# Splitting three output stores by partition count in a one-core tree-attention kernel

## The chip, the core and the metric

The kernel runs on one core of a Trainium2 chip. The metric is the time of one execution on the device in microseconds (us): the median of the runs of a kernel. Beside the plain runs there is one profiled execution, from which all views of the profile come.

## What is computed

Inputs are Q, K and V of shape 8 x 12 x 512 x 64 in float32, so 96 heads of 512 rows of 64 numbers. The output has the same shape and type.

```python
mask[i, j] = 1 where j is i or an ancestor of i in a binary tree   # parent = (i - 1) // 2
scores = einsum('bhqd,bhkd->bhqk', Q, K) / sqrt(64) + (1 - mask) * (-1e9)
weights = exp(scores - max(scores));  weights /= sum(weights) + 1e-10
return einsum('bhqk,bhkd->bhqd', weights, V)
```

## The kernel before

The 96 heads are worked through in 48 pairs (`NP` = 48). The main loop runs over i from 0 to 48. For each pair, TensorE transposes Q and K (`turn`), makes two sets of scores (`scores1`, `scores2`), ScalarE takes their exponentials, TensorE multiplies with V (`values`), and VectorE divides by the row sums into an output tile (`norm`, the instructions of line 693). All of this is written out by hand in one order per engine; there is no scheduler.

An output tile `of` holds eight heads, 128 partitions and 4 x 64 float32 numbers (1 KB) for each head and partition. From pair 16 on, pair i holds heads 8 * (i // 4) + i % 4 and that number plus 4. So pairs 36 to 39 fill the tile of heads 72 to 79, pairs 40 to 43 that of heads 80 to 87, and pairs 44 to 47 that of heads 88 to 95.

The loads and most of the stores are issued by GpSimd (POOL) through its software queue, q0 in the profile. They are listed in `pool_program` and issued in that order as soon as `ready` allows. The loads come first. The stores follow in steps of eight heads, 1 MB each. For the tile of heads 72 to 79, POOL stores only heads 72 to 75 (512 KB); the store of heads 80 to 87 (1 MB) is its last.

SyncE (SP) issues the other stores through a hardware queue, q1 in the profile:

- after step i = 41 (`APART_AT`), heads 76 to 79 (`APART`), which the change's name calls pairs 38 and 39 by size: 4 heads, 512 KB, in two stores of 60 and 68 partitions, that is 240 KB and 272 KB (`store_apart`, line 711);
- after steps 45, 46 and 47, the heads of pairs 44, 45 and 46: 256 KB each, all 128 partitions (line 885);
- at the end, one head of pair 47 (128 KB, line 887). Its other head is stored by ScalarE through its own hardware queue, q10 (line 888).

Every store goes through the helper `store`, so all have line 701 in the profile. Each waits for the VectorE instruction that wrote the last of its heads; the stores of one engine are issued in the order written. Every packet of q1 and of q10 that carries data is 1 KB: one head of one partition.

Of the kernel before, what the change touches and what calls it, by code (L numbers as in the profile page):

```python
# [119 lines left out]
def kernel(  # L120
# [7 lines left out]
    nc = tc.nc  # L128
    B, H, S, D = Q.shape
    P = nc.NUM_PARTITIONS  # L130
# [4 lines left out]
    NP = 2 * NQ  # L135
# [134 lines left out]
    def head(i, a):  # L270

        if i >= FAR:
            return 8 * (i // 4) + i % 4 + 4 * a
        return 2 * i + a if i < WIDE else 4 * (i // 2) + i % 2 + 2 * a
# [275 lines left out]
    def turn(name, i):  # L550
        pairs = range(i, i + (2 if i >= WIDE else 1))
        if name == "qst" and i >= FAR:
            pairs = range(i - i % 4, i - i % 4 + 4)
        assert all((name, head(j, a)) in issued for j in pairs for a in range(2)), (name, i)
        level = (i >= WIDE) + (i >= FAR)
        {"kst": (narrow_k, wide_k, wide_k), "qst": (narrow_q, wide_q, far_q)}[name][level](i)
        return i + (2 if i >= WIDE else 1)
# [4 lines left out]
    def scores1(i):  # L562

        sp = psS.tile([P, 2, 512], fp32, name="s1")
        for a in range(2):
            nc.tensor.matmul(  # L566
                out=sp[:, a, :],
                lhsT=(k1code if i < WIDE else k1wide)[64 * a:64 * a + CODE_ROWS, :],
                rhs=(q1code, q1wide, q1far)[(i >= WIDE) + (i >= FAR)][64 * a:64 * a + CODE_ROWS],
                start=True, stop=False,  # L570
            )
        for a in range(2):
            nc.tensor.matmul(  # L573
                out=sp[:, a, :], lhsT=keys(i, a, TOP),
                rhs=qTs[i][64 * a:64 * a + 64, :, :].rearrange("p t c -> p (t c)"),
                start=False, stop=True,
            )
        et = etpool.tile([P, 2, 4, 128], bf16, name="e1")
        nc.scalar.activation(  # L579
            out=et[:, :, :, :].rearrange("p a t c -> p (a t c)"),  # L580
            in_=sp[:, :, :].rearrange("p a c -> p (a c)"),
            func=AF.Exp, scale=scale,
        ) if i < WIDE else nc.scalar.activation(  # L583
            out=et[:, :, :, :].rearrange("p a t (r u) -> p a (t r) u", u=2 if i < FAR else 4),
            in_=sp[:, :, :].rearrange("p a (u c) -> p a c u", u=2 if i < FAR else 4),
            func=AF.Exp, scale=scale,
        )
        ets[i] = et
# [34 lines left out]
    def scores2(i):  # L623
        if i >= WIDE:
            return scores2_wide(i)
        sp = psS.tile([P, 2, 4, 128], fp32, name="s2")
        flat = sp[:, :, :, :].rearrange("p a t c -> p a (t c)")
        for a in range(2):
            nc.tensor.matmul(
                out=sp[:, a, :, 32:128], lhsT=k2code[64 * a:64 * a + CODE_ROWS, :],  # L630
                rhs=q2code[64 * a:64 * a + CODE_ROWS, :].rearrange(
                    "p (t c) -> p t c", t=4
                )[:, :, 32:128],
                start=True, stop=False,
            )
        for t, lo, hi in ((2, 32, 192), (0, 192, 256), (3, 288, 448), (1, 448, 512)):
            for a in range(2):
                nc.tensor.matmul(
                    out=flat[:, a, lo:hi], lhsT=keys(i, a, TILE2[t]),
                    rhs=qTs[i][64 * a:64 * a + 64, :, :].rearrange("p t c -> p (t c)")[:, lo:hi],  # L640
                    start=False, stop=t == 1, skip_group_check=t in (2, 3),
                )
        nc.scalar.activation(
            out=e2s[i % NE][:, :, :, 32:128].rearrange("p a t c -> p (a t) c"),
            in_=sp[:, :, :, 32:128].rearrange("p a t c -> p (a t) c"),
            func=AF.Exp, scale=scale,
        )

    def values(i):

        if i < NP - 1:
            obs[i] = ob = psO.tile([P, 2, 512], fp32, name="ob")
        else:
            obs[i] = ob = psS.tile([P, 2, 512], fp32, name="s1")
        e1, e2, vt = ets[i], e2s[i % NE], vts[(head(i, 0) // VB) % NV]

        vtile = VTILE if i < WIDE else WVTILE
        assert all(("vt", n, head(i, a)) in issued for n in PARTS[(i >= 8) + (i >= 16)] for a in range(2))

        def product(e, a, t, tile_v, lo=0, hi=128, **flags):  # L660
            nc.tensor.matmul(  # L661
                out=ob[lo:hi, a, 65 * t:65 * t + 65],
                lhsT=e[:, a, PLACE[t], lo:hi],
                rhs=vt[vtile[tile_v][0]][:, head(i, a) % VB, vtile[tile_v][1], 0:D + 1],
                **flags,
            )

        def halves(a):
            for t in (0, 1):
                product(e2, a, t, 1 + SELF[t], 0, 64, start=False, stop=t == 1)  # L670
                product(e2, a, t, 1 + t, 64, 128, start=False, stop=t == 1)

        for a in range(2):
            for t in range(4):
                product(e1, a, t, 0, start=t == 0, stop=False)
            for t in (2, 3):
                product(e2, a, t, 1 + t, start=False, stop=False)
            if i == NP - 1:
                halves(a)
        if i < NP - 1:  # L680
            for a in range(2):
                halves(a)

    def norm(i):
        j, r = divmod(i, 4)
        if r == 0:
            ofs[j] = opool.tile([P, 8, 4, D], fp32, name="of")
        o4 = obs[i][:, :, 0:260].rearrange("p a (t c) -> p a t c", c=D + 1)
        rec = small.tile([P, 2, 4, 1], fp32, name="rec")
        for a, n in ((0, 2),) if i < NP - 1 else ((0, 1), (1, 1)):  # L690
            nc.vector.reciprocal(out=rec[:, a:a + n, :, :], in_=o4[:, a:a + n, :, D:D + 1])  # L691
            h0, h1 = [head(i, x) % 8 for x in (a, a + n - 1)]
            nc.vector.tensor_tensor(  # L693
                out=ofs[j][:, h0:h1 + 1:head(i, 1) - head(i, 0), :, :],
                in0=o4[:, a:a + n, :, 0:D],
                in1=rec[:, a:a + n, :, :].to_broadcast([P, n, 4, D]),
                op=ALU.mult,
            )

    def store(eng, h0, n, step=1, p0=0, p1=P):  # L700
        return eng.dma_start(  # L701
            out=Or[p0:p1, h0:h0 + step * (n - 1) + 1:step, :],
            in_=ofs[h0 // 8][p0:p1, h0 % 8:h0 % 8 + step * (n - 1) + 1:step, :, :].rearrange(
                "p h t d -> p h (t d)"
            ),
        )


    APART, APART_AT, APART_ROWS = 76, 41, 60

    def store_apart():

        for p0, p1 in ((0, APART_ROWS), (APART_ROWS, P)):
            store(nc.sync, APART, 4, 1, p0, p1)

    def pool_program():
# [135 lines left out]
    for i in range(NP + 1):  # L852
        steps = FIRST[i] if i < len(FIRST) else "SVK" if i % 2 else "SVQ"
        steps = "SQVK" if i == FAR - 1 else steps
        for step in steps:
            if step == "S" and i < NP:
                scores1(i)
                scores2(i)
            if step == "V" and i >= 1:
                values(i - 1)  # L860
                norm(i - 1)
                valued = True
            if step == "K" and kdone < NP:
                kdone = turn("kst", kdone)
            if step == "Q" and qdone < NP:
                qdone = turn("qst", qdone)
            if step == "W":
                nc.scalar.copy(
                    out=codes[64:64 + CODE_ROWS, 1280:1536], in_=codes[0:CODE_ROWS, 1280:1536]
                )  # L870
            if step == "X":
                spin("s1" if valued else "ob", 2)
            if step == "D":
                spread_by(nc.vector.tensor_copy, BY_VECTOR, STEADY_VECTOR, i)
            if step == "A":
                spread_by(nc.scalar.copy, BY_SCALAR, STEADY_SCALAR, i)
        if "D" not in steps:
            spread_by(nc.vector.tensor_copy, BY_VECTOR, STEADY_VECTOR, i)
        if "A" not in steps:
            spread_by(nc.scalar.copy, BY_SCALAR, STEADY_SCALAR, i)  # L880
        pool(i)
        if i == APART_AT:
            store_apart()
        if i >= NP - 3 and i < NP:
            store(nc.sync, head(i - 1, 0), 2, 4)
    assert not program
    store(nc.sync, head(NP - 1, 0), 1)
    store(nc.scalar, head(NP - 1, 1), 1)
# [30 lines left out]
```

## Time and profile before

| | us |
|---|---|
| median of 3 plain runs | 134.24 (134.17 to 134.83) |
| the profiled execution's own time | 135.14 |
| its span, first to last instruction | 133.4 |

The profiled execution took 0.90 us more than the median, and 1.7 us of its time lie outside the span. In the views, q0 is the queue of POOL's transfers (loads and stores), q1 that of SP, q10 that of ScalarE, and q8 and q14 fetch instructions. "DMA share" is the mean busy share of the core's 16 DMA engines. Packets are noted with a small overlap, so the share of a stretch in which all 16 work without a break can pass 1.

### The profile page before, as it was taken

The numbers are of one execution on the slowest core, as the hardware profiler recorded it, in microseconds if no ns is written. First come the engines' busy times: TensorE is split into PE (matmuls) and PEld (weight loads), VectorE is DVE, ScalarE is ACT, GpSimd is POOL, SyncE is SP. The second block draws the span as 40 slices with busy tenths as digits, with TensorE's granted clock in tenths as the row PEclk, the third lists the DMA queues.
The fourth block names the chain that finished last, engine by engine and source line by source line (L and its number), as shares of the span: only waits on it lengthen the run. The fifth ranks groups of instructions, "written<-read, shape, count | busy, mean of one in ns | idle before, by whom it ended". The sixth has DMA issues, their size and how long they took to land.

```text
span 133.4 us, 5419 instructions
## 1 busy us (share of the span) xinstructions
PE 112.9 (85%) x2350; PEld 79.2 (59%) x2353; DVE 105.2 (79%) x254; ACT 98.6 (74%) x159; POOL 85.0 (64%) x116
## 2 busy tenths in 40 slices
PE   6786989599899889899989898995999999999700
PEld 2343665467577567576757666763766777766500
DVE  3439779988999998889889699996999977783610
ACT  4359578579779796689976977974999778889500
POOL 6989639454573999995599999728998644002000
PEclk9999999999999999999999999999999999999955
DMA  2999999999999999999999999999999999999970
GB/s 97 243 179 195 201 196 200 201 206 202 200 204 211 202 209 204 210 207 202 208 205 205 341 231 204 333 241 288 287 248 325 220 360 402 403 397 367 356 266 14
DMA packets 28092, 32.25 MB, mean 242 GB/s; under 512 B 1149, under 2 KB 23293, under 8 KB 28069
## 3 DMA queue, kind: packets, MB, share of 16 engines
q0 software_dynamic: 25696, 29.63, 109.5%
q1 hardware_dynamic: 1813, 1.83, 4.0%
q10 hardware_dynamic: 560, 0.46, 1.1%
q8 instruction: 18, 0.29, 0.8%
q14 instruction: 5, 0.04, 0.1%
HBM read 37.94 MB, written 12.58 MB: 379 GB/s over the span
## 4 chain that ended last, share of the span: by engine, by line
DMA 29%; DVE 23%; POOL 19%; PE 18%; issue 5%; ACT 2%; POOLq 0%; ACTq 0%
DMA vst<-in_V_dram 15%; DMA qst<-in_Q_dram 14%; POOL vt L370 10%; DVE vt L370 8%; PE ob L661 7%; DVE of L693 6%; POOL kst L243 2%; PE s L566 2%; POOL qst L243 2%; DVE rec L691 2%; PE ktp L469 2%; PE s L573 1%; DVE kq L485 1%; ACT e L617 1%; PE s L600 1%
## 5 line engine op out<-in xcount | busy, mean ns | idle before, releaser
L583 ACT ACTIVATE e<-s 128x1024 bf16<-128x1024 f32 x40 | 40.9, 1023 | 16.1 <-PE s L573 15.8
L661 PE MATMUL ob<-vt,e 128*128 128x65 bf16 (+1 forms) x940 | 37.2, 197 | 2.0 <-DVE of L693 1.5
L661 PEld LDWEIGHTS <-e 128*128 128x128 bf16 (+1 forms) x960 | 30.2, 102 | 10.4 <-DVE of L693 2.2
L370 POOL COPY vt<-vst 32x512 int32<-32x512 int32 (+4 forms) x44 | 32.2, 733 | 4.9 <-PE ob L661 2.7
L617 ACT ACTIVATE e<-s 128x384 bf16<-128x384 f32 x80 | 34.7, 491 | 0.0
L693 DVE TENSOR_TENSOR of<-ob,rec 128x512 f32<-128x512 f32 x47 | 32.5, 691 | 1.6
L370 DVE COPY vt<-vst 32x1024 bf16<-32x1024 bf16 (+5 forms) x47 | 23.2, 493 | 3.0 <-DMA vst<-in_V_dram 2.2
L691 DVE RECIPROCAL rec<-ob 128x8 f32<-128x8 f32 x47 | 9.6, 204 | 10.2 <-PE ob L661 9.0
L701 POOL DMA_DIRECT2D out_dram<-of x11 | 9.8, 890 | 9.2 <-DVE of L693 8.8
L611 PEld LDWEIGHTS <-kq 64*128 64x128 bf16 x320 | 12.2, 94 | 5.2 <-issue 0.7
L573 PE MATMUL s<-qq,kq 64*128 64x512 bf16 x80 | 15.3, 377 | 0.0
L611 PE MATMUL s<-qq,kq 64*128 64x64 bf16 (+1 forms) x320 | 14.9, 208 | 0.4 <-issue 0.4
L566 PE MATMUL s<-far,codes 40*128 40x512 bf16 x64 | 12.5, 386 | 0.1
L579 ACT ACTIVATE e<-s 128x1024 bf16<-128x1024 f32 x8 | 8.2, 1022 | 5.9 <-PE s L573 5.9
L542 DVE COPY qq<-qtp 128x1024 bf16<-128x1024 bf16 x16 | 10.9, 681 | 1.4 <-PE qtp L537 1.4
L253 POOL DMA_DIRECT2D qst<-in_Q_dram x12 | 8.5, 705 | 4.7 <-DMA kst<-in_K_dram 1.8
L600 PEld LDWEIGHTS <-codes 40*128 40x128 bf16 x80 | 6.1, 95 | 8.7 <-issue 3.2
L370 ACT COPY vt<-vst 32x512 int32<-32x512 int32 (+3 forms) x19 | 10.4, 545 | 1.2 <-DMA vst<-in_V_dram 0.8
L476 PE MATMUL ktp<-ptile,kst 128*64 128x128 bf16 x256 | 10.1, 220 | 1.0 <-issue 0.6
L600 PE MATMUL s<-far,codes 40*128 40x384 bf16 x64 | 10.6, 324 | 0.4 <-ACT e L617 0.3
L253 POOL DMA_DIRECT2D kst<-in_K_dram x11 | 8.4, 762 | 3.6 <-DMA vst<-in_V_dram 1.9
L298 POOL DMA_DIRECT2D vst<-in_V_dram x7 | 5.8, 823 | 5.8 <-DMA vst<-in_V_dram 4.0
(56 smaller groups left out, 153.6 us busy)
## 6 DMA issues: line engine op xcount, KB each, us to landing
out_dram<-of POOLq DMA_DIRECT2D x10, 1024.0 KB, 15.8
kst<-in_K_dram POOLq DMA_DIRECT2D x9, 512.0 KB, 14.4
qst<-in_Q_dram POOLq DMA_DIRECT2D x8, 512.0 KB, 16.3
vst<-in_V_dram POOLq DMA_DIRECT2D x12, 256.0 KB, 13.5
vst<-in_V_dram POOLq DMA_DIRECT2D x6, 512.0 KB, 12.8
qst<-in_Q_dram POOLq DMA_DIRECT2D x6, 256.0 KB, 12.3
kst<-in_K_dram POOLq DMA_DIRECT2D x4, 256.0 KB, 9.7
out_dram<-of SPq DMA_DIRECT2D x3, 256.0 KB, 6.9
```

The costliest lines, as they stand in the source:

```text
L253: return nc.gpsimd.dma_start(out=kept[b][:, h0 % KB:h0 % KB + n, :, :].rearrange("p (g x) t d -> p g (x t d)", x=x), in_=src[:, h0 // x:(h ...
L370: return copy(out=dst, in_=src)
L542: nc.vector.tensor_copy(out=qqs[j][:, :, 8 * last:8 * last + 8, :].rearrange("p b u c -> p b (u c)"), in_=quarters,)
L566: nc.tensor.matmul(out=sp[:, a, :], lhsT=(k1code if i < WIDE else k1wide)[64 * a:64 * a + CODE_ROWS, :], rhs=(q1code, q1wide, q1far)[(i >= ...
L573: nc.tensor.matmul(out=sp[:, a, :], lhsT=keys(i, a, TOP), rhs=qTs[i][64 * a:64 * a + 64, :, :].rearrange("p t c -> p (t c)"), start=False, ...
L583: ) if i < WIDE else nc.scalar.activation(
L600: nc.tensor.matmul(out=flat[:, a, :, :].rearrange("p u (t c) -> p u t c", t=4)[:, :, :, 32 // n:], lhsT=k2wide[64 * a:64 * a + CODE_ROWS, ...
L611: nc.tensor.matmul(out=flat[:, a, :, lo:hi], lhsT=keys(i, a, WTILE2[t]), rhs=qT[64 * a:64 * a + 64, :, lo:hi], start=False, stop=t == 1, s ...
L617: nc.scalar.activation(out=e2s[i % NE][:, a, :, 32:128].rearrange("p t (r u) -> p t r u", u=n), in_=flat[:, a, :, :].rearrange("p u (t r) ...
L661: nc.tensor.matmul(out=ob[lo:hi, a, 65 * t:65 * t + 65], lhsT=e[:, a, PLACE[t], lo:hi], rhs=vt[vtile[tile_v][0]][:, head(i, a) % VB, vtile ...
L691: nc.vector.reciprocal(out=rec[:, a:a + n, :, :], in_=o4[:, a:a + n, :, D:D + 1])
L693: nc.vector.tensor_tensor(out=ofs[j][:, h0:h1 + 1:head(i, 1) - head(i, 0), :, :], in0=o4[:, a:a + n, :, 0:D], in1=rec[:, a:a + n, :, :].to ...
```

## The change

The store of heads 76 to 79 is issued by SP in three pieces of 36, 24 and 68 partitions in place of two of 60 and 68. The store of pair 44 is issued in two pieces of 108 and 20 partitions in place of one of 128. The bytes and the instructions of the other engines stay. SP issues eight stores in place of six. The transfers of the two hardware queues take eight completion semaphores in turn, and one that takes a semaphore for the second time first waits for the transfer that had it. With two more transfers these places shift by two: the store of 20 partitions and SP's three later stores each wait for one of the four transfers at the start of the kernel, and ScalarE's last store waits for the landing of the new store of 36 partitions.

```diff
-    APART, APART_AT, APART_ROWS = 76, 41, 60
+    APART, APART_AT, APART_ROWS = 76, 41, (36, 60, P)
 
     def store_apart():
 
-        for p0, p1 in ((0, APART_ROWS), (APART_ROWS, P)):
+        for p0, p1 in zip((0,) + APART_ROWS, APART_ROWS):
             store(nc.sync, APART, 4, 1, p0, p1)
...
         if i >= NP - 3 and i < NP:
-            store(nc.sync, head(i - 1, 0), 2, 4)
+            for p0, p1 in ((0, 108), (108, P)) if i == NP - 3 else ((0, P),):
+                store(nc.sync, head(i - 1, 0), 2, 4, p0, p1)
```

## The prediction

> **What bounds the kernel now.** I began with the table by stages, because the change touches only stores that are issued after 111 us. Its columns: the stretch, its length, busy us (and instructions) of PE, PEld, DVE, ACT and POOL, granted clock, DMA share, GB/s.
>
> ```profile
> 115.00:119.00 4.00, 3.93 (x79) 2.93 (x77) 3.07 (x8) 3.23 (x7) 0.00 (x0) 1.00 1.04 403
> 119.00:121.00 2.00, 1.82 (x36) 1.18 (x37) 0.87 (x2) 2.00 (x4) 0.80 (x1) 1.00 1.00 386
> 121.00:122.00 1.00, 1.00 (x18) 0.51 (x14) 0.88 (x2) 0.83 (x3) 0.11 (x1) 1.00 0.88 329
> 122.00:124.00 2.00, 1.88 (x40) 1.16 (x35) 0.92 (x3) 1.97 (x4) 0.00 (x0) 1.00 1.02 372
> 124.00:126.50 2.50, 1.86 (x44) 1.42 (x40) 1.46 (x5) 1.30 (x3) 0.00 (x0) 1.00 0.99 358
> 126.50:128.70 2.20, 0.00 (x0) 0.00 (x0) 0.56 (x3) 0.00 (x0) 0.00 (x0) 0.59 0.98 348
> 128.70:129.30 0.60, 0.00 (x0) 0.00 (x0) 0.00 (x0) 0.00 (x0) 0.00 (x0) 0.50 0.55 191
> 129.30:130.30 1.00, 0.00 (x0) 0.00 (x0) 0.00 (x0) 0.00 (x0) 0.00 (x0) 0.50 0.25 85
> 130.30:131.80 1.50, 0.00 (x0) 0.00 (x0) 0.00 (x0) 0.00 (x0) 0.00 (x0) 0.50 0.06 23
> 131.80:133.40 1.60, 0.00 (x0) 0.00 (x0) 0.00 (x0) 0.00 (x0) 0.00 (x0) 0.50 0.00 0
> ```
>
> The last columns carry the argument. The 16 DMA engines are full until 121, dip to 0.88 for one microsecond, and are nearly full again until 128.7. TensorE has nothing left from 126.5. Then the DMA share falls to 0.55, to 0.25, and to 0.06. One engine of 16 is 0.0625, so from 130.3 to 131.8 a single DMA engine works and all else has ended. The end of the kernel is the moment at which the most loaded DMA engine has written its last packet. In the last 1.6 us nothing moves: that is the landing and the closing of the program, which the change does not touch.
>
> The queue's own waits from 122 on say the same of SP:
>
> ```profile
> engine line waited for: us in total, times, longest us
> SPq L701 <- DVE of L693: 12.1, 3, 9.8
> SPq L914 <- DMA out_dram<-of: 4.5, 3, 2.1
> ```
>
> Line 914 is the end of the program. SP waits there for stores to land. Before that it waits for VectorE, and once for 9.8 us.
>
> Next, what each store is, and how long from issue to landing:
>
> ```profile
> out_dram<-of SPq DMA_DIRECT2D x3, 256.0 KB, 6.9
> ...
> out_dram<-of SPq DMA_DIRECT2D x1, 272.0 KB
> ...
> out_dram<-of SPq DMA_DIRECT2D x1, 240.0 KB, 7.9
> out_dram<-of SPq DMA_DIRECT2D x1, 128.0 KB, 5.5
> out_dram<-of ACTq DMA_DIRECT2D x1, 128.0 KB, 4.7
> ```
>
> The 240 KB store (60 partitions) was issued at 111.2 and landed 7.9 us later, at 119.1. The third of SP's stores, that of pair 44, waits for VectorE until 122 (the timeline's line further below). So all q1 packets between 119 and 121 belong to the store of 68 partitions, give or take one:
>
> ```profile
> q0 software_dynamic: 193, 0.73, 93.6%
> q1 hardware_dynamic: 42, 0.04, 6.0%
> ```
>
> These are packets, MB, and the share of 16 engines in those 2 us, 32 us of engine time. A q0 packet takes 93.6% of 32 over 193 = 0.155 us; a q1 packet 6.0% of 32 over 42 = 46 ns. An engine that takes the two queues in turn needs 0.20 us for one of each, so it writes 9.9 q1 packets in 2 us. Then 42 packets are the work of about four engines: the 68-partition store runs on four of them, 17 partitions and 68 KB each. Sixty-eight is not divisible by 16; its largest divisor up to 16 is 4. I take this as the pattern: a store runs on as many engines as the largest such divisor. The Trainium skill's page "DMA: Bandwidth & Descriptors", section "Why a DMA increments its semaphore by 16 and not by 1", states it as the rule, and adds that the hardware path takes the lowest-numbered engines; the trace agrees on four, and no row here names an engine.
>
> **The change, part by part.** By that pattern, in KB for each engine that takes part:
>
> - Heads 76 to 79 before: 60 partitions of 4 KB on 15 engines, 16 each; 68 on 4, 68 each. After: 36 on 12 engines, 12 each; 24 on 12, 8 each; 68 as before.
> - Pair 44 before: 128 partitions of 2 KB on 16 engines, 16 each. After: 108 on 12, 18 each; 20 on 10, 4 each.
>
> An engine that takes part in every piece carried 16 + 68 + 16 = 100 KB and now carries 12 + 8 + 68 + 18 + 4 = 110 KB: ten more packets. One that takes part in none of the new pieces loses 32 KB, or 16 KB if it had none of the 60-partition store. The change moves work from a few engines to most of the others.
>
> What is it worth? Only the engine that ends last counts. No row tells which it is. The four with the 68-partition store stand out: apart from that store all engines are given almost the same, and the 68 KB are 68 x 46 ns = 3.1 us of an engine's time. Other things spread the engines too, since that tail is single, not four wide. I take the last engine to be one of the four and to take part in every piece.
>
> An engine that works without a break until its end is later by what it is given more, in whatever order the queues take it. The price of a q1 packet, low end, from the engine that is alone at the end (130.3 to 131.8):
>
> ```profile
> DMA packets 37, 0.03 MB, mean 23 GB/s; under 512 B 4, under 2 KB 37, under 8 KB 37
> q1 hardware_dynamic: 28, 0.03, 4.9%
> q10 hardware_dynamic: 9, 0.01, 1.6%
> ```
>
> Four of the 37 are the small ones that report an end, so 33 packets of data in 1.5 us, 45 ns each. High end, from the crowded stretch 122.8 to 124.4, where these packets would be written:
>
> ```profile
> q1 hardware_dynamic: 106, 0.11, 23.0%
> ```
>
> That is 23.0% of 25.6 us over 106, 56 ns: beside other work some q1 packets are slowed. So ten packets cost 0.45 to 0.56 us. Part of the ten go out in the crowd, part behind it; I take 0.50 us.
>
> The two added issues cost SP time:
>
> ```profile
> L701 SPq DMA_DIRECT2D out_dram<-of x6: 360/485/996, 111.2 to 126.6; - x6
> ...
> 111.24 11.21 SPq L701 DMA_DIRECT2D out_dram<-of  x3
> ...
> 123.87 3.61 SPq L701 DMA_DIRECT2D out_dram<-of  x3
> ...
> 127.12 0.35 ACTq L701 DMA_DIRECT2D out_dram<-of  x1
> ```
>
> One is 0.36 to 1.0 us, 0.49 as a median; the lines of the timeline below it put the first three between 111.24 and 122.45 and the next at 123.87. The first lies ahead of SP's wait of 9.8 us for VectorE: it delays the 68-partition store's issue, which has q0's packets ahead of it anyway. The second follows pair 44's first piece, which is issued by 122.45, and lies ahead of SP's next wait for VectorE, until 123.87. Both are hidden; without that cover 0.5 us each, but the last store's issue is not what ends. The waits on reused semaphores are for transfers of the kernel's start, and ScalarE's last store, at 127.1, waits for the 36-partition store, which should land near 119 as the 240 KB store does. Cost nothing; if the 36-partition store landed after 127.1, ScalarE's store would be late by the rest.
>
> Sum: 10 packets x 50 ns = +0.50 us. The profiled execution, 135.14 with a span of 133.4, would become 135.64 and 133.9. The median is 134.24, 0.90 below that execution; the same addition gives 134.74 us.
>
> **The rivals.** *Faster: the last engine is among those that lose.* If the engine that ends alone takes part in none of the new pieces, it loses up to 32 packets x 45 ns = 1.44 us. Then the engines that were next decide. The row 129.3 to 130.3 (share 0.25, four engines' worth) says that they end near 130.3, 1.5 us before the last. If one of these takes part in every piece it ends at 130.3 + 0.45, so the gain is 131.8 - 130.75 = 1.05 us: 133.2. For it: a single late engine, where four have the 68 KB, may be late for a reason of its own. Against it: the extra load of the four. Decided by whether the last engine is given the new pieces.
>
> *Slower: the crowd.* Fewer engines take more, and a store of 108 partitions reads its rows through 12 engines in place of 16, while POOL's last megabyte is still being written. If that slows the last engine's packets by the 10 ns between the crowded row and the earlier one, for half of its 110 packets, 0.55 us come on top of the 0.50: 135.3. For it: the price did rise from 46 to 56 ns when the store of pair 44 joined. Against it: bytes and rows stay the same in all. It decides once q1 packets cost more than 56 ns from 122 to 126.5.
>
> *No change.* The smaller pieces may be spread over all 16 engines, or the last engine's end may be set by something else; then 134.2. The same page's section "Rules for kernel authors" calls two transfers to disjoint halves of the partitions not worth it, since they use the same engines; by that rule the time stays too, or pays only for the issues. Four engines for 68 partitions speak against reading it so here.
>
> **How the numbers follow.** About 0.5% (0.67 us) is what a measurement of this kernel can tell from no change. Forecast, 0.47: own range +0.3 to +0.9 (134.5 to 135.1), since the four engines' packets may cost more than 56 ns; of this 0.27 within 0.5% and 0.20 above. Faster, 0.29: 132.9 to 133.5, all counted as faster. Crowd, 0.19: 135.0 to 135.8, slower. No change, 0.05. So faster 0.29, same 0.32, slower 0.39. The range leaves out a tenth at each side: 133.1 to 135.6. The time is that of the likeliest case.
>
> **What would show it.** In the profile after, q1's bytes stay and the issue table shows stores of 144, 96, 272, 216 and 40 KB. Right: DMA share near 1 until 128.7 but a tail at 0.06 that lasts some 2 us and ends near 132.3; q1 at 46 to 56 ns. Wrong, rival one: the tail at 0.06 is gone or short and the span is near 132.4. Wrong, rival two: q1 above 56 ns from 122 to 126.5. If the 36-partition store is no longer in flight by 119 and the tail has not moved, the count of engines for each piece is wrong.

## The result and the profile after

The changed kernel took 135.43 us (median of 6, 135.27 to 135.61) and the kernel before 134.24 (134.08 to 134.83): ratio 1.0084, 95% interval 1.0064 to 1.0105. It is slower by 1.1 us, or 0.84%; the prediction was +0.50 us and 134.74. Single executions of the kernel before, and of the variants below, are at times longer by up to 4%, mostly with a lower granted clock, and each ratio leaves out executions more than 1.5% above the fastest of their kernel.

The profiled execution after took 135.32 us with a span of 133.5, almost the same as the one before (135.14 and 133.4). So the two profiles do not show the 1.1 us as a difference of spans, and they must not be subtracted. The table by stages of the kernel after says why (columns as before: stretch, length, busy us of PE, PEld, DVE, ACT, POOL, granted clock, DMA share, GB/s):

```profile
24.00:28.00 4.00, 3.06 (x44) 1.95 (x45) 3.35 (x10) 1.34 (x4) 1.59 (x3) 0.72 1.35 199
28.00:32.00 4.00, 3.73 (x84) 2.87 (x81) 2.60 (x8) 2.85 (x4) 1.91 (x3) 0.85 1.29 206
...
122.00:124.00 2.00, 1.84 (x36) 1.16 (x34) 0.79 (x3) 1.95 (x4) 0.91 (x1) 1.00 0.59 214
124.00:126.50 2.50, 2.38 (x48) 1.55 (x46) 1.35 (x3) 2.35 (x4) 0.00 (x0) 1.00 0.95 365
126.50:128.70 2.20, 1.79 (x40) 1.35 (x40) 1.23 (x4) 1.23 (x3) 0.00 (x0) 1.00 0.75 243
...
129.30:130.30 1.00, 0.00 (x0) 0.00 (x0) 0.22 (x1) 0.00 (x0) 0.00 (x0) 1.00 1.00 353
130.30:131.80 1.50, 0.00 (x0) 0.00 (x0) 0.00 (x0) 0.00 (x0) 0.00 (x0) 0.92 0.40 140
```

TensorE still works until after 126.5 here, where before it had ended by then. The DMA engines, full before from 122 on, are only 0.59 busy from 122 to 124: they wait for stores that are not yet issued. ScalarE's last store is issued at 129.6, before at 127.1. Part of the cause lies 100 us earlier: from 24 to 32 us TensorE's clock was granted at 0.72 and 0.85 in place of 1.00. The half clock that makes these shares lasted 2 x (0.28 + 0.15) x 4 = 3.4 us, which can cost TensorE at most half of that, 1.7 us. The seventh instruction of line 693 starts at 31.2 us before and at 32.8 after, 1.6 us later. The rest of the 2.4 us arose later, at full clock, and is not explained. The stores that the change touches are issued after 113 us, and by then the arithmetic is 2.4 us late already, so this cannot be their work. The next section shows that the half clock comes and goes.

The stores are split as intended:

```profile
out_dram<-of SPq DMA_DIRECT2D x1, 272.0 KB
...
out_dram<-of SPq DMA_DIRECT2D x1, 216.0 KB
out_dram<-of SPq DMA_DIRECT2D x1, 144.0 KB
...
out_dram<-of SPq DMA_DIRECT2D x1, 96.0 KB
...
out_dram<-of SPq DMA_DIRECT2D x1, 40.0 KB
```

How many engines carry the pieces can be counted. SP's stores are 1408 KB in both kernels, so they make 1408 packets of data. What q1 has beyond these are the small packets that report an end, 4 bytes each. From 108 us to the end, before and after:

```profile
q1 hardware_dynamic: 1491, 1.44, 16.6%
...
q1 hardware_dynamic: 1506, 1.44, 16.6%
```

That leaves 83 before, 15 + 4 + 4 x 16, and 98 after, 12 + 12 + 4 + 12 + 10 + 3 x 16: one for each engine of each store, with the numbers of engines that the prediction assumed. The sum comes out in the profiles of all the runs below too.

The issues of SP and of ScalarE, shortest, median and longest in ns, and the first and last:

```profile
L701 SPq DMA_DIRECT2D out_dram<-of x8: 304/396/2501, 113.7 to 129.0; - x8
L701 ACTq DMA_DIRECT2D out_dram<-of x1: 351/351/351, 129.6 to 129.6; - x1
```

SP's longest took 2.5 us, where before it was 1.0.

### The profile page after: what moved, and what is told of

It is laid out like the page before. It is cut to its first block, busy times and chain, and to the rows that moved or that the text cites. A ratio compares the mean times of both kernels' runs of the same rounds, so it can differ in the third digit from the quotient of the medians.

```text
span 133.5 us, 5425 instructions
## 1 busy us (share of the span) xinstructions
PE 114.7 (86%) x2353; PEld 80.2 (60%) x2353; DVE 105.5 (79%) x254; ACT 98.6 (74%) x159; POOL 85.2 (64%) x116
## 4 chain that ended last, share of the span: by engine, by line
PE 45%; DVE 25%; ACT 7%; DMA 7%; issue 7%; POOL 6%; ACTq 0%; POOLq 0%
PE ob L661 15%; DVE vt L370 9%; DMA vst<-in_V_dram 7%; DVE of L693 6%; PE s L566 6%; PE s L573 4%; ACT e L617 4%; PE s L611 4%; PE s L600 4%; PE ktp L476 4%; PE qtp L537 3%; ACT e L583 3%; POOL kst L243 2%; POOL qst L243 2%; DVE rec L691 2%
## 5 line engine op out<-in xcount | busy, mean ns | idle before, releaser
L661 PE MATMUL ob<-vt,e 128*128 128x65 bf16 (+1 forms) x940 | 37.8, 198 | 3.4 <-DVE of L693 1.4
L661 PEld LDWEIGHTS <-e 128*128 128x128 bf16 (+1 forms) x960 | 30.7, 103 | 11.5 <-issue 2.1
L611 PE MATMUL s<-qq,kq 64*128 64x160 bf16 (+1 forms) x320 | 14.8, 208 | 0.4 <-issue 0.4
L485 DVE COPY kq<-ktp 128x256 bf16<-128x256 bf16 x20 | 8.3, 416 | 2.3 <-PE ktp L476 2.2
```

Source lines behind the costliest of these rows:

```text
L611: nc.tensor.matmul(out=flat[:, a, :, lo:hi], lhsT=keys(i, a, WTILE2[t]), rhs=qT[64 * a:64 * a + 64, :, lo:hi], start=False, stop=t == 1, s ...
L661: nc.tensor.matmul(out=ob[lo:hi, a, 65 * t:65 * t + 65], lhsT=e[:, a, PLACE[t], lo:hi], rhs=vt[vtile[tile_v][0]][:, head(i, a) % VB, vtile ...
```

## The experiments

**The kernel before again, and the two halves.** Four kernels on one chip, beside the same runs of the kernel before (median 134.33). The first has no edit.

> The kernel before, unchanged, for a second profile of it and a ratio that should be 1. The two profiles differ in more than the stores: in the one after, TensorE's granted clock is 0.72 from 24 to 28 us in place of 1.00, and from there on all arithmetic is later, by 2.43 us at the end (ScalarE's last store is issued at 129.56 in place of 127.12). Theory 'bytes': the measured +1.19 us is the last DMA engine's ten more packets, +0.5, and something on top; then this profile repeats the first one's tail (last issue near 127.1, a DMA share of 0.06 for 1.5 us). Theory 'clock': the dip at 25 us comes and goes between executions of any of these kernels, and this profile may show it. Theory 'clock by program': the dip belongs to the changed program, and this profile shows none. Ratio 1.000 under all.

Ratio 0.9994 (0.9972 to 1.0016). The profiled execution, of 136.52 us, has half clock too, in an earlier place:

```profile
0.00:24.00 24.00, 18.79 (x248) 10.83 (x249) 14.15 (x42) 12.59 (x18) 18.63 (x28) 0.86 1.26 188
24.00:28.00 4.00, 3.90 (x86) 2.73 (x84) 3.85 (x10) 3.93 (x6) 1.52 (x3) 1.00 1.33 198
```

0.86 over 24 us is 2 x 0.14 x 24 = 6.7 us of half clock, about twice the 3.4 of the kernel after; it lies from 11.5 to 18.3 us, and a further 3.4 us at 0.50 follow from 49.1. Its last store was issued at 130.9. So the unchanged kernel has such windows too, and "clock by program" falls. The Trainium skill's page "TensorE: Matmul & The Clock Gate", section "Part 1: The HAM clock gate (the 'warmup' mystery)", describes a gate that watches TensorE over windows of about 3.4 us and halves the clock after an idle one; the lengths here agree with whole windows. But the windows ahead of the half clock are not idle here: TensorE was busy for 1.84 of 3.41 us ahead of it in the first profile after, and for 1.97 and 1.65 of 3.41 us in this one.

The first half of the change alone:

```diff
-    APART, APART_AT, APART_ROWS = 76, 41, 60
+    APART, APART_AT, APART_ROWS = 76, 41, (36, 60, P)
...
-        for p0, p1 in ((0, APART_ROWS), (APART_ROWS, P)):
+        for p0, p1 in zip((0,) + APART_ROWS, APART_ROWS):
```

> The store of heads 76 to 79 in 36, 24 and 68 partitions, that of pair 44 whole. Theory 'bytes': the last engine has 4 KB more (12 + 8 in place of 16), so +0.2 us, ratio 1.0015. Theory 'clock by program': if the dip at 25 us is in this profile, the time is near the changed kernel's, +1.2 us, ratio 1.009, and if it is not, near 1.000. Theory 'issue': one more store in a queue that waits anyway, nothing.

Ratio 1.0036 (1.0002 to 1.0070), +0.48 us. Its profiled execution has a dip as well, 0.86 and 0.71 from 24 to 32 us.

The second half alone:

```diff
-            store(nc.sync, head(i - 1, 0), 2, 4)
+            for p0, p1 in ((0, 108), (108, P)) if i == NP - 3 else ((0, P),):
+                store(nc.sync, head(i - 1, 0), 2, 4, p0, p1)
```

> The store of pair 44 in 108 and 20 partitions, that of heads 76 to 79 in 60 and 68. Theory 'bytes': the last engine has 6 KB more (18 + 4 in place of 16), so +0.3 us, ratio 1.002. Theory 'clock by program': +1.2 us with the dip in the profile, 0 without. Theory 'issue': the second piece's issue took 2.50 us in the profile of the changed kernel (from 124.83) where the others took 0.3 to 0.5; if that, and not the bytes, makes the end late, this kernel has the whole +1.2 us and the one with only heads 76 to 79 split has none.

Ratio 1.0044 (1.0017 to 1.0071), +0.59 us. Each half costs, and the two add up to the whole, 1.1 us. The intervals reach down to 0.03 and 0.23 us, so the 0.2 and 0.3 of the theory "bytes" are not excluded. Its profile, without a dip, is the nearest to the first one of the kernel before:

```profile
126.50:128.70 2.20, 0.00 (x0) 0.00 (x0) 0.38 (x1) 0.00 (x0) 0.00 (x0) 0.56 0.95 338
...
129.30:130.30 1.00, 0.00 (x0) 0.00 (x0) 0.00 (x0) 0.00 (x0) 0.00 (x0) 0.50 0.16 54
130.30:131.80 1.50, 0.00 (x0) 0.00 (x0) 0.00 (x0) 0.00 (x0) 0.00 (x0) 0.50 0.03 12
```

TensorE is done by 126.5 and one engine is alone at the end again, with less of a lag: 0.03 x 16 x 1.5 = 0.7 us after 130.3. This single execution (134.45 us) was shorter than that first one of before (135.14). One profile of each kernel does not rank changes of this size.

As many stores as in the changed kernel, which the diff is against, but the old bytes on each engine:

```diff
-    APART, APART_AT, APART_ROWS = 76, 41, (36, 60, P)
+    APART, APART_AT, APART_ROWS = 76, 41, (45, 60, P)
...
-            for p0, p1 in ((0, 108), (108, P)) if i == NP - 3 else ((0, P),):
+            for p0, p1 in ((0, 64), (64, P)) if i == NP - 3 else ((0, P),):
```

> As many stores as in the changed kernel, but each engine with the bytes it had before: heads 76 to 79 in 45, 15 and 68 partitions (12 + 4 in place of 16 KB on fifteen engines), pair 44 in 64 and 64 (8 + 8 in place of 16 KB on sixteen). Theory 'bytes': ratio 1.000. Theory 'issue' (the added stores, their waits and the later issues cost, not the bytes): near the changed kernel's 1.008. Theory 'clock by program': 1.000 or 1.009, with the dip's absence or presence in the profile.

Ratio 1.0009 (0.9990 to 1.0027). Two more stores, their waits on reused semaphores and the longer issues cost at most 0.36 us, and 0.1 as it was measured. SP's issues were stretched here as well:

```profile
L701 SPq DMA_DIRECT2D out_dram<-of x8: 350/623/1720, 113.8 to 129.2; - x8
```

So theory "issue" falls: it is how the pieces spread over the engines that costs, not that there are more of them. Pieces of 108 and 20 partitions differ from these in their shape as well as in KB for each engine, and the last experiment comes back to that.

**The changed kernel again, a steadier clock, and even bytes.** Beside runs of the kernel before with a median of 134.28. The first has no edit against the changed kernel.

> The changed kernel again, on the same chip and beside the same runs as the next three. So far it was 1.008 of the kernel before, the two halves alone 1.004 each, and the kernel with the same number of stores and the old bytes per engine 1.001. Theory 'bytes': 1.005 to 1.008 again. Theory 'clock' (the difference of the first two profiles, 2.43 us in the arithmetic, is chance: one execution with a window of half clock near 25 us, one without): the time of this kernel varies as much as that of the kernel before, and the window may lie elsewhere or be absent in this profile.

Ratio 1.0048 (1.0021 to 1.0076), +0.64 us. This profile has no dip, and the last store of ScalarE is issued at 128.2:

```profile
24.00:28.00 4.00, 2.72 (x62) 2.00 (x63) 3.72 (x11) 2.19 (x4) 2.10 (x4) 1.00 1.34 200
...
129.30:130.30 1.00, 0.00 (x0) 0.00 (x0) 0.00 (x0) 0.00 (x0) 0.00 (x0) 1.00 0.76 265
130.30:131.80 1.50, 0.00 (x0) 0.00 (x0) 0.00 (x0) 0.00 (x0) 0.00 (x0) 0.69 0.09 33
131.80:134.00 2.20, 0.00 (x0) 0.00 (x0) 0.00 (x0) 0.00 (x0) 0.00 (x0) 0.50 0.01 2
```

The clock is full, and the tail of about one engine is back: 0.09 in the stretch where before it was 0.06. In the last row one engine works on past 131.8, where before all was quiet; its last packet ends at 132.0, before at 131.8. Even without a dip the arithmetic is 1.1 us later here than in the first profile before (ScalarE's last store at 128.2 against 127.1), so this end is not the work of the change alone. The price of its q1 packets from 122 to 126.5:

```profile
q1 hardware_dynamic: 306, 0.31, 21.1%
```

21.1% of 72 us over 306 is 50 ns, as in the kernel before in the same stretch (26.8% over 383 packets).

Idle matmuls against the dips, in both kernels:

```diff
-    FIRST = ['KSQ', 'SXKQXDVAKQ', 'SVKQ', 'SKQAV', 'KSVXQA', 'SAKQVDW', 'SKDVQ', 'SVD', 'SVDKQX']
+    FIRST = ['KSQ', 'SXKQXDVAKQ', 'SXVKQX', 'SKXQAVX', 'KSVXQAX', 'SXAKQVDWX', 'SKXDVQX', 'SXVD', 'SVDKQX']
```

> The kernel before, with nine more pairs of idle matmuls on TensorE (step X) in the loop's steps 2 to 7, where windows of half clock were seen; all else is as before. Theory 'clock': the profile has a granted clock of 1.00 from 14 to 32 us, the last store is issued near 127 us, and the runs scatter less than those before (which go from 133.8 to 138.5); the median moves by less than 0.5 us. If the added matmuls are not hidden, the arithmetic comes up to 4 us later and the time rises by what is not absorbed by the loads.

> The changed kernel with the same added idle matmuls. Against the one before it this is the bytes alone, without the scatter of the clock, if the matmuls do what they are meant to. Theory 'bytes': later than the kernel of label e6_before_steady by 0.45 to 0.56 us if the price of the prediction holds (45 to 56 ns a packet), by 1.1 us if the measured price holds (110 ns). Theory 'clock': no difference between the two beyond 0.2 us.

Both missed. The profiles have a granted clock of 0.9 or more in every slice up to the end, but the added matmuls were not hidden: ratios 1.0461 (1.0409 to 1.0513) and 1.0497 (1.0441 to 1.0552) to the kernel before. Their ratios differ by 0.5 us, inside the width of either interval, so this pair says nothing on the change.

Even bytes:

```diff
-    APART, APART_AT, APART_ROWS = 76, 41, 60
+    APART, APART_AT, APART_ROWS = 76, 41, 64
```

> Heads 76 to 79 in 64 and 64 partitions, each on sixteen engines by the pattern: 32 KB on every engine, in place of 84 on four, 16 on eleven and 0 on one. Nothing else changes. If the four engines with the 68 KB end last (the prediction's choice), they lose 52 KB, 2.3 us at 45 ns, and the end falls to the next engines, which gain 16 or 32 KB, 0.7 to 1.4 us: by the first profile, where these end near 130.3, 131.0 to 131.7 in place of 131.8, so 0.1 to 0.8 us faster. If the last engine is another, it gains 16 KB or 32 KB: 0.7 to 1.4 us slower, and the prediction's choice was wrong.

Ratio 1.0025 (0.9996 to 1.0054). Neither forecast came out: +0.34 us (-0.05 to +0.73), no gain, and half of the smaller loss. The profile shows two late engines in place of one:

```profile
129.30:130.30 1.00, 0.00 (x0) 0.00 (x0) 0.00 (x0) 0.00 (x0) 0.00 (x0) 1.00 0.35 121
130.30:131.80 1.50, 0.00 (x0) 0.00 (x0) 0.00 (x0) 0.00 (x0) 0.00 (x0) 0.77 0.10 34
```

0.10 x 16 x 1.5 = 2.4 us of work after 130.3 is more than one engine can do in 1.5. With the same bytes on every engine some still end 1.5 us after the rest. So engines differ by something else than SP's stores, and taking the heavy load from four is of no use while others get 16 or 32 KB more. POOL's last store tells the same: two of its sixteen shares landed at 129.3 and 129.6, the other fourteen by 127.5.

**The dose, and a better split.** Beside runs of the kernel before with a median of 134.18. First, the changed kernel with its new split for three pairs:

```diff
-            for p0, p1 in ((0, 108), (108, P)) if i == NP - 3 else ((0, P),):
+            for p0, p1 in ((0, 108), (108, P)) if i <= NP - 1 else ((0, P),):
```

> The changed kernel, with the stores of pairs 45 and 46 in 108 and 20 partitions too: an engine that takes part in every piece gets 4 + 3 x 6 = 22 KB more than before in place of 10. This is the dose that the noise between executions does not cover. Theory 'bytes' at the prediction's price, 45 to 56 ns a packet: +1.0 to +1.2 us on the kernel before, ratio 1.0075 to 1.009. At twice that, as the first comparison of before and after looked: +2.4 us, 1.018. If the changed kernel's loss is from something else than the bytes of the loaded engines (the seven more issues of SP apart): near 1.005.

Ratio 1.0105 (1.0059 to 1.0151), +1.41 us for 22 KB: 64 ns for each KB, with 36 to 92 by the interval, so the 45 to 56 of the prediction are within it. (SP issues ten stores here, four more than the kernel before and not seven.)

Then, from the kernel before, all of heads 76 to 79 on four engines:

```diff
-    APART, APART_AT, APART_ROWS = 76, 41, 60
+    APART, APART_AT, APART_ROWS = 76, 41, 124
```

> Heads 76 to 79 in 124 and 4 partitions, both on four engines by the pattern (31 x 4 and 4 x 1): 128 KB on each of four engines in place of 84, nothing on the other twelve in place of 16 on eleven of them. Pair 44 is whole. Theory 'bytes', the last engine being one of the four: +44 KB at 45 to 56 ns, +2.0 to +2.5 us, ratio 1.015 to 1.018. If the last engine is one of the other twelve: faster by up to 0.7 us (16 KB) until the four overtake it.

Ratio 1.0125 (1.0073 to 1.0177), +1.68 us for 44 KB. The q1 packets from 119 to 121, and the end:

```profile
q1 hardware_dynamic: 40, 0.04, 5.8%
...
128.70:129.30 0.60, 0.00 (x0) 0.00 (x0) 0.00 (x0) 0.00 (x0) 0.00 (x0) 0.50 0.50 176
129.30:130.30 1.00, 0.00 (x0) 0.00 (x0) 0.00 (x0) 0.00 (x0) 0.00 (x0) 0.50 0.30 107
130.30:131.80 1.50, 0.00 (x0) 0.00 (x0) 0.00 (x0) 0.00 (x0) 0.00 (x0) 0.50 0.27 94
131.80:134.00 2.20, 0.00 (x0) 0.00 (x0) 0.00 (x0) 0.00 (x0) 0.00 (x0) 0.50 0.07 26
```

40 packets in 2 us, as for 68 partitions (42). The share is 0.27, four engines of 16 and a little, until 131.8: four engines end last, with the other twelve idle. One issue of SP is stretched as nowhere else:

```profile
L701 SPq DMA_DIRECT2D out_dram<-of x6: 286/1334/10277, 111.1 to 126.7; - x6
```

That of the four partitions, issued behind the 124, took 10.3 us. It goes to the four engines that still have the 124 KB each to write; that their queues were full is likely, but no view shows it.

Next, from the kernel before, a split that takes load from the four and gives none to four others:

```diff
-    APART, APART_AT, APART_ROWS = 76, 41, 60
+    APART, APART_AT, APART_ROWS = 76, 41, 108
```

> Heads 76 to 79 in 108 and 20 partitions: 36 + 8 = 44 KB on ten engines, 36 on two, nothing on four, in place of 84 on four, 16 on eleven, 0 on one. Pair 44 is whole. The kernel with 32 KB on all sixteen was no better than before, with two late engines in its profile in place of one. Theory 'one slow engine outside the loaded ones, and the four with 84': this relieves both, and the end falls to the engines between, which gain 28 KB, 1.3 us, on an end near 129.3 to 130.2 in the first profile: 130.6 to 131.5 in place of 131.8, so 0.3 to 1.2 us faster, ratio 0.991 to 0.998. Theory 'the engines between are late enough': same or up to 0.5 us slower.

Ratio 0.9951 (0.9921 to 0.9981): 133.56 us, faster than the kernel before by 0.66 us, and the best of all. The tail has gone:

```profile
128.70:129.30 0.60, 0.00 (x0) 0.00 (x0) 0.00 (x0) 0.00 (x0) 0.00 (x0) 1.00 0.82 285
129.30:130.30 1.00, 0.00 (x0) 0.00 (x0) 0.00 (x0) 0.00 (x0) 0.00 (x0) 0.67 0.14 46
130.30:131.80 1.50, 0.00 (x0) 0.00 (x0) 0.00 (x0) 0.00 (x0) 0.00 (x0) 0.50 0.00 0
```

All engines end within about 1 us, by 130.3, and the shares of POOL's last store end without a straggler (127.6 and 127.8 are the last two). Against even bytes (1.0025) it differs in the four engines that get nothing from heads 76 to 79, and in the 4 to 12 KB more on the others.

And the change's second half on top of it, again against the kernel before:

```diff
-    APART, APART_AT, APART_ROWS = 76, 41, 60
+    APART, APART_AT, APART_ROWS = 76, 41, (108, P)
...
-            store(nc.sync, head(i - 1, 0), 2, 4)
+            for p0, p1 in ((0, 108), (108, P)) if i == NP - 3 else ((0, P),):
+                store(nc.sync, head(i - 1, 0), 2, 4, p0, p1)
```

> Heads 76 to 79 in 108 and 20 partitions, as in the kernel that was 0.995 of the one before, and pair 44 in 108 and 20 too, the change's second half. The four engines with 84 KB are gone, and the profile's tail with them: the second half puts 6 KB on engines that are no longer alone at the end and takes 16 KB from four others. If the second half costs by its bytes on whatever engine ends last: at most 6 x 45 to 56 ns, +0.3 us on the kernel of label e11_twelve, ratio to the kernel before 0.997. If it cost 0.3 to 0.6 us only because of the four engines: 0.995 again. If its own shape costs (two issues, 108 rows through 12 engines) apart from that: 0.999.

Ratio 0.9991 (0.9944 to 1.0037), median 134.05. It lies nearest to the third expectation, that the second half costs by its own shape, but the interval holds all three. A little work is back after 129.3:

```profile
129.30:130.30 1.00, 0.00 (x0) 0.00 (x0) 0.00 (x0) 0.00 (x0) 0.00 (x0) 0.99 0.20 69
130.30:131.80 1.50, 0.00 (x0) 0.00 (x0) 0.00 (x0) 0.00 (x0) 0.00 (x0) 0.50 0.01 3
```

## Why the prediction was right or wrong

*The bound* was read rightly for the execution in the first profile: the most loaded DMA engine sets the end. It holds less widely than the prediction took it. In the first profile after, late arithmetic left the DMA engines partly idle from 122 to 124, which the prediction, with one profile, could not know.

*The pattern of engines* held for every piece: the counts of small packets give 15, 12, 10 and 4 engines where the prediction put them, and with 124 and 4 partitions four engines are alone at the end (0.27 for 1.5 us).

*The last engine* being one of the four is borne out. The trace of the kernel before keeps when each engine's share of a store landed: the four shares of the 68 partitions at 124.4, 125.0, 125.3 and 126.9 us. From then on each store of SP and ScalarE has one share that lands 1.5 to 1.6 us behind the next. So one of the four was already 1.6 us behind the other three, although by the pattern all four had the same 84 KB, and the equal lag says that it is this engine that ends last: it is late for a reason of its own, as the first rival supposed, and carries the extra load too. POOL's last store shows the same lag, with one share at 129.7 and the other fifteen by 128.2. In the second profile of the kernel before the four landed together (124.7 to 125.1), and yet one share of the next store came 2.0 us behind the rest; which engine that was, no view tells. That the loaded engines matter, the times show: 44 KB more on four cost 1.68 us, 22 KB more on the engines that take part in every piece 1.41, and spreading the load of the four over more engines gained 0.66. But the choice was not the whole: even bytes gained nothing.

What makes single engines late was not tested. One candidate is the fetching of instructions: a 16 KB packet of q8 in the stretch from 122 to 126.5 took 1.3% of 72 us, 0.94 us of one engine's time. No view tells which engine carries it.

*The size* is the weak step: ten packets at 50 ns, +0.50 us, against +1.13 (0.86 to 1.41) in the first comparison and +0.64 (0.28 to 1.02) in the second. The first median, 135.43, lies outside the forecast's own range (134.5 to 135.1); that it lies in the whole range, to 135.6, is luck, since it falls there among the times of the crowd, which is not what happened. The second median, 134.87, lies in the forecast's own range. The kernel before stayed between 134.18 and 134.33 in all comparisons, so it is the executions of the changed kernel that differ, and why is open. At 45 to 56 ns a KB the doses of 4, 6, 22 and 44 KB and the second comparison reach into their intervals; in the first comparison it lies below. The small doses lean high (0.48 us for 4 KB, 0.59 for 6) and the large one low (38 ns a KB for 44). Whether there is something of 0.1 to 0.6 us beside the bytes is left open; the shape of the pieces is a candidate (0.9991 against 0.9951, with intervals that overlap). It is not the number of stores (1.0009).

*The added issues* were sized at 0.5 us and took up to 2.5. That they are hidden held: 1.0009 with issues of up to 1.7 us. That ScalarE's last store does not wait held too: the last share of the 36 partitions landed at 120.8, that store was issued at 129.6.

*The rivals.* Faster, because the last engine loses: wrong for this change, though unloading the four engines does help once four others are relieved (0.9951). Slower by the crowd, with q1 packets over 56 ns: not seen, 50 ns from 122 to 126.5 in the second profile after and in the kernel before. No change: excluded by both comparisons. The Trainium skill's page "DMA: Bandwidth & Descriptors", section "Rules for kernel authors", speaks of halves, which both spread over all 16 engines. For 64 and 64 partitions in the store of pair 44 the run agrees (1.0009); most pieces here go to 4, 10, 12 or 15 engines, and by their partition counts alone the splits move the time from 0.995 to 1.0125.

*What would show it*: a tail of 2 us by one engine was not in the first profile after. It is there in the second, but ends at 132.0 and not near 132.3.

## What to carry to other kernels

Where a kernel ends in a drain of stores, read the DMA share of the last microseconds times 16: it says how many engines are still at work, and a tail of one to four is time that a better spread of the same bytes may win back. Here the partition count of a store decided how many engines carried it, so choose the pieces by their divisors and count KB for each engine over all pieces. Then measure: 108 and 20 in place of 60 and 68 brought 0.5%, while 64 and 64, the even spread, brought nothing. For changes of less than 1% compare many executions: one profile of each kernel can differ by chance by more than the change.

## What was not expected of the hardware

Windows of half clock early in the run, 3.4 and 6.8 us long, come and go between executions of the same kernel, and follow stretches of 3.4 us in which TensorE was busy for about half of the time (1.65 to 1.97 us). Behind a store with 124 KB on each of four engines, SP's next issue took 10.3 us. With equal bytes from SP on all 16 engines, two ended 1.5 us and more after the rest.
